# DeltaNet: beta and decays ahead of the first convolution; Q loaded back for its norms among the inverses; gates stored from ScalarE's queue

## The chip, the cores and the metric

The kernel runs on one core of a Trainium2 chip, as one program. The metric is the device time of one execution in microseconds (us); lower is better. Five engines work side by side, and each runs its own instructions strictly in the order in which they were written: TensorE (PE) multiplies matrices, VectorE (DVE) and ScalarE (ACT) work on elements, GpSimd (POOL) does some elementwise work, and SyncE (SP) mainly issues transfers (DMAs). ACT can issue transfers too, between its other instructions.

## What is computed

A decoder trunk of two layers on 16 meta tokens and 512 real ones with 1024 features: retention, then gated DeltaNet, each followed by a dense SwiGLU feed-forward network, all in float32. The change touches the DeltaNet layer alone. Cut to what matters, the reference has, for 8 heads with keys of 128 and values of 256 features:

```
qkv = silu(causal_conv(h @ w_in[qkv], conv_w))       # four taps along the tokens
q = l2norm(q) * DN_DK ** -0.5 ; k = l2norm(k)
beta = sigmoid(h @ w_in[beta])
g = -exp(a_log) * softplus(h @ w_in[a] + dt_bias)
# per chunk of tokens:
gam = cumsum(g) ; decay = exp(gam_i - gam_j) where i >= j
a_mat = strictly lower part of beta * (k k^T) * decay
u, w = triangular_solve(I + a_mat, [v * beta, k * beta * exp(gam)])
v_new = u - w @ state
o = (q * exp(gam)) @ state + ((q k^T) * decay) @ v_new
state = state * exp(g_last) + (k * exp(g_last - gam))^T @ v_new
y = (o / rms(o)) * norm_w * silu(h @ w_in[gate])   ;   out = y @ w_out
```

## The kernel before

Every large product splits both operands into a rounded part and a rest (`xhi`, `xlo` for the tokens, `whi`, `wlo` for the weights) and adds three products. A weight tile of 128x1024 is loaded by SP as `wraw`, cast to `whi` by ACT (line 179), and the rest `wlo` is formed by DVE (line 180); there are three buffers of each. TensorE multiplies at line 470 into a PSUM tile `g`, of which there are two. A weight tile's product with all 528 tokens is 48 matmuls of 264 columns.

The order of the instructions on each engine is fixed when the program is written: the code is a set of generators with due times (`spawn`, `tick`, the constants at the top), and a list scheduler then sets each engine's order. On the chip nothing is reordered.

The DeltaNet layer has these stages, in time: the keys and queries of 8 heads (`dn_keys`), the value products of the first heads, the gate products (`dn_silu_gate`), then the recurrence (`dn_states`, `dn_scan`) among further value and gate products.

- **Keys stage.** The products of head 0 are made as a pair (`gemm_pair`). Each product is scaled into `pad` by DVE (line 1202), convolved by ACT (first tap, line 1205) and DVE (three taps, line 1207), and passed through Silu on ACT (line 1210). The result goes to the DRAM scratch `d_kq` and is cast to `z` (line 460). For each head, the query's copy is also transposed by TensorE (`dn_norms`, line 1396, four transposes) and squared with a running sum by ACT (line 1400), which gives the query norms in `eq`.
- **Gates for beta and decay** (`dn_gates`). A product of 48 columns (line 1235), a few small products, a store to the scratch `d_g` and loads of it into tiles `zh` and `zl` per head, an addition on POOL (line 1356) that masks, and per head and chunk an exponential on ACT (line 1363), 32 in all. Silu and Exp sit in different tables of ACT, so each change from one to the other has an ACT_TABLE_LOAD.
- **Attention of a head** (`dn_attention`). Products of keys with keys and queries, which need `dec` (the exponentials) and `km`; they end in `d_mp`, the matrices to be inverted.
- **Inverse** (`dn_inverse`). All blocks are inverted at once by substitution on DVE (lines 1472 and 1478). The results go back to DRAM (`d_x`, `d_mp`, `d_m1`) by SP and ACT (lines 1496, 1497, 1501). Then `d_m1` is loaded into `rr` three times (line 1505, twice from SP and once from ACT's queue), cast to `um` by ACT (line 1506). The merge of the first two heads (`dn_merge`) loads `wh` from `d_x` (line 1515), transposes it on DVE into `wl` (line 1516) and multiplies on TensorE (line 1526) with `z`, loaded from `d_kq` and `d_mp` (lines 1720, 1721). ACT copies the product to `rh` (line 1534).
- **Output gates** (`dn_silu_gate`). 48 matmuls of 512 columns for each of two weight tiles, a scaling on DVE (line 1606), a Silu on ACT (line 1607) and a store to `d_sg` by SP (line 1608). Four of the eight gates stand ahead of the merge.

Of the kernel before, what the change touches and what calls it, by code (L numbers as in the profile page):

```python
# [10 lines left out]
AF = mybir.ActivationFunctionType  # L11
ALU = mybir.AluOpType
PSUM = bass.MemoryType.PSUM

P = 128
D = 1024
KT = D // P
NM = 16
NT = 512
T = NM + NT  # L20
HH = T // 2
EPS = 1e-6

RH = 4
DH = 8
# [18 lines left out]
TO_ATTEND = 7  # L44
ROWS = 5
POW = 5
NORMS = 18
ATTEND = 13
ATTEND_LAST = 8
ROWS_IN = (2, 10)  # L50
PAIRS_APART = 14
MASKED = 4
VALUES = 6
GATE_STEPS = (3, 6, 3)
GATES = [2, 2, 0, 2]
# [4 lines left out]
class Hybrid:  # L60
# [1130 lines left out]
    def conv_silu(self, w, x, rb, mt):  # L1191

        nc = self.nc
        p = self.psum_g()
        self.gemm(p, w, x, range(KT))
        return self.conv_evac(p, rb, mt)

    def conv_evac(self, p, rb, mt):
        nc = self.nc
        self.pads.reverse()  # L1200
        pad = self.pads[0]
        nc.vector.tensor_tensor(self.halves(pad[:, 3 : 3 + T]), p[:, :, :HH], self.halves(rb), op=ALU.mult)
        acc = self.t(self.tp, [P, T], "ra", bufs=4)
        cw = self.convw
        nc.scalar.activation(acc, pad[:, :T], AF.Copy, scale=cw[:, mt, 0:1])
        for i in range(1, 4):
            nc.vector.scalar_tensor_tensor(  # L1207
                acc, pad[:, i : i + T], cw[:, mt, i : i + 1], acc, op0=ALU.mult, op1=ALU.add
            )
        nc.scalar.activation(acc, acc, AF.Silu)  # L1210
        return acc

    def dn_gates(self, sp, x, rb):


        nc, a = self.nc, self.a
# [11 lines left out]
        pick = self.t(gp, [48, 16], "pick")  # L1228
        nc.vector.tensor_copy(pick, self.ident[:48, :16])
        nc.vector.tensor_copy(pick[32:48], self.ident[32:48, 32:48])  # L1230
        p = self.psum_g()
        for kt in range(KT):
            for i in range(2):
                for half in range(2):
                    nc.tensor.matmul(
                        p[:48, half, :HH],
                        wst[:, kt, :],
                        x[i][:, kt, half * HH : half * HH + HH],
                        start=kt == 0 and i == 0,
                        stop=kt == KT - 1 and i == 1,  # L1240
                    )
        ba = self.t(self.tp, [P, T], "ra", bufs=4)[:48]
        nc.vector.tensor_tensor(self.halves(ba), p[:48, :, :HH], self.halves(rb[:48, :]), op=ALU.mult)
        bm = self.t(self.tp, [P, 96], "am", bufs=1)
        nc.gpsimd.memset(bm, 0.0)
        self.spread(bm[:48], ba[:, :NM])
# [1 line left out]
        pt = self.psum_m()  # L1248
        for ch in range(5):
# [5 lines left out]
        ax, xa, e, z, z2, q = (  # L1255
            tmp[:, 80 + 40 * i : 120 + 40 * i].rearrange("p (a b) -> p a b", b=DH) for i in range(6)
        )
# [43 lines left out]
        pt = self.psum_m()  # L1301
# [6 lines left out]
        def rows_in(pair):  # L1308
            for hd in (2 * pair, 2 * pair + 1):
                self.dec[hd] = self.t(sp, [P, 4, P], ("zh", "zl")[pair % 2], bufs=3)  # L1310
                nc.sync.dma_start(self.dec[hd], by_head[hd, 1:].unsqueeze(0).to_broadcast([P, 4, P]))
# [5 lines left out]
        for dst, mat, meta in ((self.eglast, self.ones, self.ones[:NM, :]), (self.ekw, self.later, later3)):  # L1317
# [14 lines left out]
            op=ALU.mult,  # L1332
# [13 lines left out]
        for pair in range(DH // 2):  # L1346
            hds = (2 * pair, 2 * pair + 1)
            if pair == 1:
                yield PAIRS_APART
            if pair > 0:  # L1350
                while self.attended < 2 * (pair - 1):
                    yield 1
                rows_in(pair)
            yield ROWS_IN[pair > 0]
            for hd in hds:
                nc.gpsimd.tensor_tensor(
                    self.dec[hd], self.dec[hd], apart.unsqueeze(1).to_broadcast([P, 4, P]), op=ALU.add
                )
            yield MASKED
            for hd in hds:  # L1360
                for c in range(4):
                    o, de = (c + 1) * DH + hd, self.dec[hd][:, c]
                    nc.scalar.activation(de, de, AF.Exp, scale=-1.0, bias=sums[:, o : o + 1])
            self.decays = 2 * pair + 2

    def dn_keys(self, pool, hd, x, rb, first, gt):

        nc, a = self.nc, self.a
        for s, base in ((1, 0), (0, 8)):
            if first is None:  # L1370
                w = self.load_w(a["w_dqk"][hd, 1 - s])
                p = self.psum_g()
                self.gemm(p, w, x, range(KT))
            else:
                p = first.pop(0)
            t_ = self.conv_evac(p, rb, base + hd)
            real = t_[:, NM:].rearrange("p (c i) -> p c i", c=4)
            nc.sync.dma_start(self.d_kq[:, hd, :, s, :], real)
            if s == 1:
                zz = self.t(pool, [P, 2, 4, 2, P], "z", F32R)  # L1380
                zh, zl = zz[:, 0], zz[:, 1]
            self.split(zh[:, :, s, :], zl[:, :, s, :], real)
            if s == 0:
                nc.vector.tensor_copy(self.kmf[:, hd, :], t_[:, :NM])
            else:
                self.spawn(self.dn_norms(hd, t_), NORMS)
        return self.spawn(
            self.dn_attention(pool, hd, zh, zl, gt), ATTEND if hd < DH - 1 else ATTEND_LAST
        )

    def dn_norms(self, hd, t_):

        nc = self.nc
        pt = self.psum_m()
        for c in range(4):
            nc.tensor.transpose(pt[:, c * P : (c + 1) * P], t_[:, NM + c * P : NM + (c + 1) * P], self.ident)
        eq = self.eq[:, hd, :]
        for c in range(4):
            jk = self.t(self.sp, [P, P], "rh")
            nc.scalar.activation(jk, pt[:, c * P : (c + 1) * P], AF.Square, accum_out=eq[:, c : c + 1])  # L1400
        yield 1
        nc.vector.tensor_scalar(eq, eq, EPS, EPS * P, op0=ALU.add, op1=ALU.mult)

    def dn_attention(self, pool, hd, zh, zl, gt):

# [192 lines left out]
    def dn_silu_gate(self, hd, x, rb):  # L1598

        nc, a = self.nc, self.a  # L1600
        p = self.psum_g()
        ws = [self.load_w(a["w_dg"][hd, i]) for i in range(2)]
        for i in range(2):
            self.gemm(p, ws[i], x, range(KT), lo=NM, bank=i)
        sg = self.t(self.gp, [P, 2, NT], "sg", bufs=2)
        nc.vector.tensor_tensor(sg, p, rb[:, NM:].unsqueeze(1).to_broadcast([P, 2, NT]), op=ALU.mult)
        nc.scalar.activation(sg, sg, AF.Silu)
        nc.sync.dma_start(self.d_sg[:, hd], sg)

    def dn_scan(self, hd, z, vs, sp):  # L1610

# [152 lines left out]
    def deltanet(self, st, ctx, nxt):  # L1764
        nc, a = self.nc, self.a
        x = (st["hi"], st["lo"])
        self.gp = gp = self.pool(ctx, "dn", 1)
        self.sp = sp = self.pool(ctx, "scan", 2)
        op = self.pool(ctx, "og", 1)
# [26 lines left out]
        def gate(n):  # L1796
            for _ in range(n):
                self.dn_silu_gate(next(gates), x, rb)
# [7 lines left out]
        first = [self.psum_g() for i in range(2)]  # L1806
        self.gemm_pair(first, ws, x)
        self.finish(rows)
        rb = st["rb"]
        gt = self.spawn(self.dn_gates(sp, x, rb))  # L1810
        for hd in range(DH):
            att = self.dn_keys(sp, hd, x, rb, first if hd == 0 else None, gt)
            if hd in KEY_GATES:
# [1 line left out]
        self.dn_values(0, x, rb, sp)  # L1815
        self.finish(att)
        inv = self.spawn(self.dn_inverse(sp))
        self.dn_values(1, x, rb, sp)
        gate(FIRST_GATES)
        self.finish(inv)  # L1820
        self.spawn(self.dn_states(sp, op))
        for pair in range(4):
            gate(GATES[pair])
# [264 lines left out]
```

## Time and profile before

| | |
|---|---|
| median of 3 runs | 1669.75 us (1668.28 to 1670.8) |
| profiled execution | 1669.76 us, of which the span from first to last instruction is 1668.0 us |
| TensorE busy | 1643.1 us, 99% of the span |
| VectorE busy | 1297.6 us, 78% |
| ScalarE busy | 886.1 us, 53% |
| mean granted TensorE clock | 0.996 of full speed |

A share of busy time is an average over all stages. The DeltaNet layer runs from about 800 us on; its keys stage lies between 800 and about 905 us, the inverse between 937 and 1004 us.

### The profile page before, as it was taken

Reading aid. Unit: us, or ns where it says so; the run is one execution under the profiler, and the core shown is the slowest. Engines: PE = TensorE matmul, PEld = TensorE weight load, DVE = VectorE, ACT = ScalarE, POOL = GpSimd, SP = SyncE. Lnnn points to the kernel's source line nnn. Section 1 sums busy time; section 2 is a strip of 40 time slices with the busy share of each in tenths; the row PEclk is TensorE's granted clock in tenths of the full one; section 3 lists DMA queues with packets and bytes.
Section 4 is the critical chain, followed back from the end, with each engine's and each line's share of the span. In section 5 each row is a group of like instructions: output and inputs, shape, how many; then the busy total and the mean of one; then the engine's idle time right before and its main releaser. Section 6 shows DMA issues by size and latency. Waiting matters only on the chain.

```text
span 1668.0 us, 30777 instructions
## 1 busy us (share of the span) xinstructions
PE 1643.1 (99%) x12415; PEld 1550.9 (93%) x12415; DVE 1297.6 (78%) x2121; ACT 886.1 (53%) x1536; POOL 99.7 (6%) x139
## 2 busy tenths in 40 slices
PE   9999999999999999999989999999999999999998
PEld 9999999999999999999989988888877889999896
DVE  7886877798698887784689888796876798888672
ACT  5445555555345545543595427776663455555542
POOL 1000000000000000000030000010100000000010
PEclk9999999999999999999999999999999999999999
DMA  6564746565323332453354554432323223333451
GB/s 211 175 165 119 219 111 198 176 210 167 113 89 102 102 102 82 122 155 101 102 158 159 140 143 139 156 104 89 107 75 114 90 89 113 102 107 110 114 163 52
DMA packets 91888, 214.54 MB, mean 129 GB/s; under 512 B 20394, under 2 KB 42146, under 8 KB 90466
## 3 DMA queue, kind: packets, MB, share of 16 engines
q1 hardware_dynamic: 80066, 194.21, 35.3%
q0 software_dynamic: 4688, 16.53, 5.7%
q10 hardware_dynamic: 6992, 1.85, 0.5%
q8 instruction: 97, 1.59, 0.4%
q14 instruction: 45, 0.37, 0.1%
HBM read 190.30 MB, written 22.25 MB: 127 GB/s over the span
## 4 chain that ended last, share of the span: by engine, by line
PE 86%; DVE 9%; ACT 3%; issue 2%; POOL 1%; POOLq 0%; ACTq 0%; DVEq 0%
PE g L470 66%; PE m L470 14%; DVE wlo L461 1%; ACT whi L460 1%; DVE wsum L220 1%; DVE ra L1207 1%; PE m L573 0%; DVE flt L461 0%; POOL ss L1686 0%; PE m L559 0%; PE m L704 0%; DVE wlo L180 0%; DVE wraw L312 0%; DVE flb L461 0%; PE m L143 0%
## 5 line engine op out<-in xcount | busy, mean ns | idle before, releaser
L460 ACT CAST whi<-wraw 128x1024 fp32r<-128x1024 f32 x171 | 179.2, 1051 | 192.5 <-PE g L470 69.4
L470 PE MATMUL g<-fht,whi 128*128 128x264 f32 (+1 forms) x976 | 277.4, 284 | 0.8 <-DVE h L338 0.7
L470 PE MATMUL g<-fht,wlo 128*128 128x264 f32 (+1 forms) x976 | 276.1, 283 | 0.8 <-DVE wlo L461 0.8
L470 PE MATMUL g<-flt,whi 128*128 128x264 f32 (+1 forms) x976 | 275.9, 283 | 0.0
L470 PE MATMUL g<-xlo,whi 128*128 128x264 f32 (+1 forms) x1088 | 260.9, 306 | 0.0
L470 PE MATMUL g<-xhi,whi 128*128 128x264 f32 (+1 forms) x1024 | 251.8, 310 | 4.6 <-ACT whi L179 4.0
L470 PE MATMUL g<-xhi,wlo 128*128 128x264 f32 (+1 forms) x1024 | 251.2, 308 | 2.3 <-DVE wlo L180 2.3
L461 DVE TENSOR_TENSOR wlo<-wraw,whi 128x1024 fp32r<-128x1024 f32 x171 | 210.5, 1234 | 46.5 <-ACT whi L460 46.2
L179 ACT CAST whi<-wraw 128x1024 fp32r<-128x1024 f32 (+3 forms) x117 | 118.1, 1011 | 138.5 <-PE g L470 107.1
L470 PEld LDWEIGHTS g<-fht,whi 128*128 128x128 f32 x976 | 183.8, 188 | 1.3 <-ACT ra L540 0.9
L470 PEld LDWEIGHTS g<-fht,wlo 128*128 128x128 f32 x976 | 183.6, 188 | 1.1 <-DVE wlo L461 1.0
L470 PEld LDWEIGHTS g<-flt,whi 128*128 128x128 f32 x976 | 183.7, 188 | 0.5
L470 PEld LDWEIGHTS g<-xlo,whi 128*128 128x128 f32 x1088 | 176.7, 189 | 7.0 <-DVE xlo L529 0.2
L470 PEld LDWEIGHTS g<-xhi,whi 128*128 128x128 f32 x1024 | 167.8, 190 | 12.4 <-ACT whi L179 4.2
L470 PEld LDWEIGHTS g<-xhi,wlo 128*128 128x128 f32 x1024 | 167.3, 189 | 10.1 <-DVE wlo L180 3.3
L180 DVE TENSOR_TENSOR wlo<-wraw,whi 128x1024 fp32r<-128x1024 f32 (+3 forms) x117 | 138.0, 1180 | 40.5 <-ACT whi L179 39.5
L470 PE MATMUL g<-fhb,whi 128*128 128x264 f32 (+1 forms) x480 | 137.4, 286 | 0.0
L470 PE MATMUL g<-fhb,wlo 128*128 128x264 f32 (+1 forms) x480 | 136.1, 284 | 1.0 <-DVE wlo L461 0.8
L470 PE MATMUL g<-flb,whi 128*128 128x264 f32 (+1 forms) x480 | 135.7, 283 | 0.0
L461 DVE TENSOR_TENSOR wlo<-wsum,whi 128x1024 fp32r<-128x1024 f32 x54 | 66.1, 1225 | 44.5 <-ACT whi L460 44.5
L470 PEld LDWEIGHTS g<-fhb,wlo 128*128 128x128 f32 x480 | 90.3, 188 | 1.8 <-DVE wlo L461 1.8
L470 PEld LDWEIGHTS g<-flb,whi 128*128 128x128 f32 x480 | 90.3, 188 | 0.5
(562 smaller groups left out, 3804.4 us busy)
## 6 DMA issues: line engine op xcount, KB each, us to landing
wraw<-in_w_gu_dram SPq DMA_DIRECT2D x66, 512.0 KB, 3.4
wraw<-in_w_ret_dram SPq DMA_DIRECT2D x56, 512.0 KB, 3.7
sraw<-in_w_gu_dram SPq DMA_DIRECT2D x22, 512.0 KB, 4.1
wraw<-in_w_ret_dram POOLq DMA_DIRECT2D x18, 512.0 KB, 5.6
wraw<-in_w_dqk_dram SPq DMA_DIRECT2D x16, 512.0 KB, 3.4
wraw<-in_w_dv_dram SPq DMA_DIRECT2D x16, 512.0 KB, 3.3
wraw<-in_w_dg_dram SPq DMA_DIRECT2D x16, 512.0 KB, 3.9
wraw<-in_w_do_dram SPq DMA_DIRECT2D x16, 512.0 KB, 3.4
```

The source lines that it names most:

```text
L179: nc.scalar.copy(hi[:, c], raw[:, c])
L180: nc.vector.tensor_tensor(lo[:, c], raw[:, c], hi[:, c].bitcast(F32), op=ALU.subtract)
L220: nc.vector.scalar_tensor_tensor(dst[:, k, :], hh[:, kb + k, cs], g[:, kb + k : kb + k + 1], rb[:, cs], op0=ALU.mult, op1=ALU.mult)
L460: self.nc.scalar.copy(hi, src)
L461: self.nc.vector.tensor_tensor(lo, src, hi.bitcast(F32), op=ALU.subtract)
L470: mm(o, l, r[which], start=first and n == 0, stop=last and n == 2, **kw)
L1207: nc.vector.scalar_tensor_tensor(acc, pad[:, i : i + T], cw[:, mt, i : i + 1], acc, op0=ALU.mult, op1=ALU.add)
```

## The change

Three things are moved. First, `dn_gates` is made right behind the pair of products of head 0: the two products are scaled into their pads, then the 48-column product is made with two small PSUM tiles (`psum_m`) in place of a large one, and two steps of the generator are taken at once; the yield of 4 ticks ahead of the exponentials is gone. Second, the query norms leave the keys stage: `dn_norms` is spawned with the inverse, loads each head's queries back from `d_kq` (8 loads of 256 KB on SP's queue), and does the same transposes and squares; one DVE instruction in place of eight ends it. Third, the store of `d_sg` is issued by ACT in place of SP.

```diff
-NORMS = 18
+NORMS = 4
...
-MASKED = 4
...
-        return self.conv_evac(p, rb, mt)
-
-    def conv_evac(self, p, rb, mt):
-        nc = self.nc
+        return self.conv_taps(self.conv_pad(p, rb), mt)
+
+    def conv_pad(self, p, rb):
         self.pads.reverse()
         pad = self.pads[0]
-        nc.vector.tensor_tensor(self.halves(pad[:, 3 : 3 + T]), p[:, :, :HH], self.halves(rb), op=ALU.mult)
+        self.nc.vector.tensor_tensor(self.halves(pad[:, 3 : 3 + T]), p[:, :, :HH], self.halves(rb), op=ALU.mult)
+        return pad
...
-        p = self.psum_g()
+        p = [self.psum_m()[:48, :HH] for half in range(2)]
...
-        nc.vector.tensor_tensor(self.halves(ba), p[:48, :, :HH], self.halves(rb[:48, :]), op=ALU.mult)
+        for half in range(2):
+            hs = slice(half * HH, half * HH + HH)
+            nc.vector.tensor_tensor(ba[:, hs], p[half], rb[:48, hs], op=ALU.mult)
...
-            yield MASKED
...
-            else:
-                self.spawn(self.dn_norms(hd, t_), NORMS)
...
+    def dn_norms(self, sp):
+
+        nc = self.nc
+
+        def load(hd):
+            q = self.t(sp, [P, 4, P], "zh", bufs=3)
+            nc.sync.dma_start(q, self.d_kq[:, hd, :, 1, :])
+            return q
+
+        qs = [load(hd) for hd in range(2)]
+        for hd in range(DH):
+            yield NORMS
+            q = qs.pop(0)
+            if hd + 2 < DH:
+                qs.append(load(hd + 2))
+            pt = self.psum_m()
+            for c in range(4):
+                nc.tensor.transpose(pt[:, c * P : (c + 1) * P], q[:, c], self.ident)
+            eq = self.eq[:, hd, :]
+            for c in range(4):
+                jk = self.t(self.sp, [P, P], "rh")
+                nc.scalar.activation(jk, pt[:, c * P : (c + 1) * P], AF.Square, accum_out=eq[:, c : c + 1])
+            yield 1
+        nc.vector.tensor_scalar(self.eq, self.eq, EPS, EPS * P, op0=ALU.add, op1=ALU.mult)
...
-        nc.sync.dma_start(self.d_sg[:, hd], sg)
+        nc.scalar.dma_start(self.d_sg[:, hd], sg)
...
+        first = [self.conv_pad(p, rb) for p in first]
+        gt = self.dn_gates(sp, x, rb)
+        for _ in range(2):
+            next(gt)
+        self.spawn(gt, GATE_STEPS[1])
...
         inv = self.spawn(self.dn_inverse(sp))
+        norms = self.spawn(self.dn_norms(sp))
...
         self.finish(inv)
+        self.finish(norms)
```

What moves shows in the order of three places. The first is ACT in the keys stage. The names are those of the list above (`rh` is what a square writes, `zh` and `zl` are decays under their exponential, `ra` a convolution). Before, from the first exponential on:

```order
L1363 ACT_TABLE_LOAD
L1363 ACTIVATE zh_9498<-zh_9498,kl_9489 128x128 x4
L1363 ACTIVATE zh_9500<-zh_9500,kl_9489 128x128 x4
L1205 ACTIVATE ra_9705<-pad_01418_9154,convw_475 128x528
L1400 ACTIVATE rh_9741,eq_9146<-m_9734 128x128
L1400 ACTIVATE rh_9743,eq_9146<-m_9734 128x128
L1400 ACTIVATE rh_9745,eq_9146<-m_9734 128x128
L1363 ACTIVATE zl_9569<-zl_9569,kl_9489 128x128 x4
L1363 ACTIVATE zl_9571<-zl_9571,kl_9489 128x128 x4
L1210 ACT_TABLE_LOAD
L1210 ACTIVATE ra_9705<-ra_9705 128x528
```

In the changed kernel, the same stretch:

```order
L178 CAST whi_9888<-wraw_9886 128x1024
L1366 ACTIVATE zh_9464<-zh_9464,kl_9455 128x128 x4
L1366 ACTIVATE zh_9466<-zh_9466,kl_9455 128x128 x4
L1212 ACT_TABLE_LOAD
L1212 ACTIVATE ra_9584<-ra_9584 128x528
L1207 ACTIVATE ra_9687<-pad_01418_9154,convw_475 128x528
L459 CAST z_9502<-ra_9584 128x4x128
L1366 ACT_TABLE_LOAD
L1366 ACTIVATE zl_9710<-zl_9710,kl_9455 128x128 x4
L1207 ACTIVATE ra_9759<-pad_01417_9153,convw_475 128x528
L1212 ACT_TABLE_LOAD
L1212 ACTIVATE ra_9687<-ra_9687 128x528
```

The squares are gone from it. From behind `whi_9888` to the next weight cast, `whi_9966`, the changed order has 24 exponentials, 6 table loads, 3 Silus, 4 first taps and 3 casts to `z`.

The second is TensorE at the first merge. Before, behind the fourth gate (`g_11568`) stand all 48 matmuls of one value product (`g_11805`) and 27 of the next, whose last rows before the merge are:

```order
L470 MATMUL g_11940<-xlo_8689,whi_11801 128x264 x2
L470 MATMUL g_11940<-xhi_8688,wlo_11802 128x264 x2
L470 MATMUL g_11940<-xhi_8688,whi_11801 128x264 x2
L470 MATMUL g_11940<-xlo_8689,whi_11801 128x264
L1526 MATMUL m_11431<-wl_11410,z_11403 64x32 x8
L470 MATMUL g_11940<-xlo_8689,whi_11801 128x264
```

In the changed kernel the fourth gate is `g_11579`, and behind its last matmul stand:

```order
L469 MATMUL g_11579<-xhi_8688,wlo_11589 128x512
L1537 MATMUL m_11442<-wl_11421,z_11414 64x32 x8
L469 MATMUL g_11816<-xhi_8688,whi_11806 128x264 x2
L469 MATMUL g_11816<-xlo_8689,whi_11806 128x264 x2
L469 MATMUL g_11951<-xhi_8688,whi_11812 128x264 x2
L469 MATMUL g_11951<-xlo_8689,whi_11812 128x264
L469 MATMUL g_11816<-xhi_8688,wlo_11807 128x264 x2
L1537 MATMUL m_11459<-wl_11432,z_11417 64x32 x8
```

The value products have moved from ahead of the merge to behind it; the eight groups of norm transposes stand further up, among the value products of heads 0 and 1 and the gates.

The third is ACT at the same place. Before, the weight casts for the value products stand ahead of the load and the cast of `um`:

```order
L1607 ACTIVATE sg_11789<-sg_11789 128x1024
L179 CAST whi_11801<-wraw_11799 128x1024
L1205 ACTIVATE ra_11934<-pad_01418_9154,convw_475 128x528
L179 CAST whi_12096<-wraw_12094 128x1024
L1505 DMA rr_11364<-d_m_01405_9140 16x128
L179 CAST whi_12102<-wraw_12100 128x1024
L1521 COPY oq_11413<-wl_11410 32x4x32 x2
L1521 COPY oq_11424<-wl_11421 32x4x32 x2
L1534 COPY rh_11440<-m_11431 128x128
L1506 CAST um_9148<-rr_11364 96x128
```

In the changed kernel:

```order
L1618 ACTIVATE sg_11800<-sg_11800 128x1024
L1619 DMA d_sg_9139<-sg_11575 128x1024
L1516 DMA rr_11375<-d_m_01405_9140 16x128
L1532 COPY oq_11424<-wl_11421 32x4x32 x2
L1532 COPY oq_11435<-wl_11432 32x4x32 x2
L1619 DMA d_sg_9139<-sg_11800 128x1024
L1517 CAST um_9148<-rr_11375 96x128
L1545 COPY rh_11451<-m_11442 128x128
L178 CAST whi_11806<-wraw_11804 128x1024
L178 CAST whi_11812<-wraw_11810 128x1024
```

`whi_11806`, the cast for the first value product behind the merge, now stands behind `um`, which reads what the transfer into `rr` brings, and behind `rh`, which reads the merge. On SP the stores of `d_sg` are gone, and the eight loads of queries stand among the weight loads of the keys stage's second half and of the first gates.

## Rows read from the trace of the kernel before

**Rows 1.** The page's busy times by engine over the whole span.

```profile
PE 1643.1 (99%) x12415; PEld 1550.9 (93%) x12415; DVE 1297.6 (78%) x2121; ACT 886.1 (53%) x1536; POOL 99.7 (6%) x139
```

**Rows 2.** What TensorE waited for, whole run: total us, times, longest.

```profile
PE g L470 <- ACT whi L179: 4.0, 1, 4.0
PE g L470 <- DVE wlo L180: 2.3, 3, 1.4
```

**Rows 3.** Stretches: length, busy us of PE, PEld, DVE, ACT, POOL; granted clock.

```profile
850.00:855.00 5.00, 3.60 (x26) 3.00 (x24) 5.00 (x11) 4.36 (x13) 0.00 (x0) 1.00 0.56 191
855.00:860.00 5.00, 4.54 (x38) 4.54 (x39) 3.37 (x13) 4.94 (x8) 0.00 (x0) 1.00 0.34 115
860.00:865.00 5.00, 2.17 (x19) 1.93 (x17) 4.83 (x16) 4.96 (x9) 1.16 (x1) 1.00 0.04 13
865.00:870.00 5.00, 3.28 (x13) 2.98 (x14) 4.91 (x11) 4.98 (x13) 0.00 (x0) 0.59 0.72 189
870.00:875.00 5.00, 5.00 (x33) 5.00 (x33) 1.71 (x2) 4.85 (x7) 1.28 (x1) 0.73 0.84 235
```

**Rows 4.** Timeline, TensorE, 856 to 867 us: start, duration, what, idle before.

```profile
856.48 0.87 PE L470 MATMUL m<-z 128*128 128x256 f32 x6
857.18 0.41 PE L470 MATMUL g<-xhi,whi 128*128 128x264 f32 x2
857.43 0.40 PE L470 MATMUL g<-xlo,whi 128*128 128x264 f32 x2
...
866.17 0.81 PE L470 MATMUL g<-xhi,whi 128*128 128x264 f32 x2 [3.99 <-ACT whi L179]
```

**Rows 5.** Timeline, ScalarE, 859 to 866 us.

```profile
860.80 1.28 ACT L1363 ACTIVATE zh<-zh,kl 128x128 f32<-128x128 f32 x4
862.10 1.28 ACT L1210 ACT_TABLE_LOAD   x1
863.39 0.64 ACT L1210 ACTIVATE ra<-ra 128x528 f32<-128x528 f32 x1
863.94 0.72 ACT L1205 ACTIVATE ra<-pad,convw 128x528 f32<-128x528 f32 x1
864.57 0.60 ACT L460 CAST z<-ra 128x512 fp32r<-128x512 f32 x1
865.08 1.04 ACT L179 CAST whi<-wraw 128x1024 fp32r<-128x1024 f32 x1
866.02 0.26 ACT L1400 ACTIVATE rh<-m 128x128 f32<-128x128 f32 x1
```

**Rows 6.** Timeline, TensorE, 846 to 1002 us: norm transposes, fourth gate's end, merge.

```profile
846.66 0.60 PE L1396 MATMUL m<-ident,ra 128*128 128x128 f32 x4
847.02 0.49 PE L470 MATMUL g<-xhi,whi 128*128 128x264 f32 x2
...
990.50 0.39 PE L470 MATMUL g<-xhi,wlo 128*128 128x512 f32 x1
...
1001.67 0.65 PE L1526 MATMUL m<-wl,z 32*64 32x32 f32 x16
```

**Rows 7.** Timelines, VectorE, ScalarE and SP's queue, 990 to 1005 us.

```profile
990.93 1.22 DVE L1606 TENSOR_TENSOR sg<-g,rb 128x1024 f32<-128x1024 f32 x1 [1.19 <-PE g L470]
...
992.25 1.06 ACT L1607 ACTIVATE sg<-sg 128x1024 f32<-128x1024 f32 x1 [9.56 <-DVE sg L1606]
997.68 0.32 ACTq L1505 DMA_DIRECT2D rr<-d_m  x1
1004.42 0.30 ACT L1506 CAST um<-rr 96x128 fp32r<-96x128 f32 x1 [1.78 <-DMA rr<-d_m]
...
994.62 0.37 SPq L1721 DMA_DIRECT2D z<-d_mp  x1
```

**Rows 8.** Transfers, 985 to 1010 us: issues, KB each, median us to landing.

```profile
z<-d_mp SPq DMA_DIRECT2D x2, 512.0 KB, 3.9
...
rr<-d_m SPq DMA_DIRECT2D x2, 8.0 KB, 3.6
```

More of the change, by code (lines that the diff above doesn't have):

```diff
@@ L1195, in conv_silu, with conv_taps @@
         self.gemm(p, w, x, range(KT))
-        return self.conv_evac(p, rb, mt)
-    def conv_evac(self, p, rb, mt):
-        nc = self.nc
+        return self.conv_taps(self.conv_pad(p, rb), mt)
+    def conv_pad(self, p, rb):
         self.pads.reverse()
         pad = self.pads[0]
-        nc.vector.tensor_tensor(self.halves(pad[:, 3 : 3 + T]), p[:, :, :HH], self.halves(rb), op=ALU.mult)
+        self.nc.vector.tensor_tensor(self.halves(pad[:, 3 : 3 + T]), p[:, :, :HH], self.halves(rb), op=ALU.mult)
+        return pad
+    def conv_taps(self, pad, mt):
+        nc = self.nc
         acc = self.t(self.tp, [P, T], "ra", bufs=4)
@@ L1235, in dn_gates @@
                     nc.tensor.matmul(
-                        p[:48, half, :HH],
+                        p[half],
                         wst[:, kt, :],
@@ L1371, in dn_keys @@
                 w = self.load_w(a["w_dqk"][hd, 1 - s])
-                p = self.psum_g()
-                self.gemm(p, w, x, range(KT))
-            else:
-                p = first.pop(0)
-            t_ = self.conv_evac(p, rb, base + hd)
+                t_ = self.conv_silu(w, x, rb, base + hd)
+            else:
+                t_ = self.conv_taps(first.pop(0), base + hd)
             real = t_[:, NM:].rearrange("p (c i) -> p c i", c=4)
@@ L1389, in dn_keys @@
         )
-    def dn_norms(self, hd, t_):
+    def dn_norms(self, sp):
         nc = self.nc
[L1394 to L1402, printed above, removed]
+        def load(hd):
[17 more added lines that the diff above has]
+        nc.vector.tensor_scalar(self.eq, self.eq, EPS, EPS * P, op0=ALU.add, op1=ALU.mult)
     def dn_attention(self, pool, hd, zh, zl, gt):
@@ L1809, in deltanet @@
         rb = st["rb"]
-        gt = self.spawn(self.dn_gates(sp, x, rb))
+        first = [self.conv_pad(p, rb) for p in first]
[3 more added lines that the diff above has]
+        self.spawn(gt, GATE_STEPS[1])
         for hd in range(DH):
```

## The prediction

> **What bounds the kernel now.** I read the page's busy times first: TensorE is busy 1643.1 of 1668.0 us [rows 1], so the time is its work plus its gaps, some 25 us over the whole run, and nothing here removes work from it. Then the list of what TensorE waited for: the longest wait is one of 4.0 us for a `whi` cast, and three waits for `wlo` add 2.3 [rows 2]. Stretches of 5 us place the first: between 850 and 870 us TensorE is busy 3.60, 4.54, 2.17 and 3.28 of each 5 us, so it idles 6.41 us, and ScalarE is busy 4.36 to 4.98 in each [rows 3]. ScalarE is what this place waits for. The idle is not all: the granted clock falls to 0.59 and 0.73 in the two stretches from 865 to 875 [rows 3]. There 13 and 33 matmuls start. At full clock a pair of 264 columns starts every 0.245 us (857.18 to 857.43 [rows 4]); the stretch from 870 to 875 would hold some 41, and it has 33, about 1 us lost, and in the 3.3 busy us from 865 to 870 at a clock of 0.59 a further 1.4 to 2. I put the clock at 2.9 us and the keys stage's loss at 9.3 us in all. The timelines then show how the wait comes about: TensorE stands 3.99 us until 866.17 [rows 4], while ScalarE does exponentials, a table load, a Silu, a first tap and a cast before the `whi` cast at 865.08 [rows 5], all in the order in which they were written.
>
> **The change, keys stage.** Away from ScalarE go the squares, four of 0.26 us per head [rows 5], about 1.0 us each for the four or five heads that lie in this stretch. The gates come earlier by the 17 matmuls that stood ahead of them (2 us), and they no longer interrupt the pair's sequence. What is left I count from the changed order, between the casts `whi_9888` and `whi_9966`: 24 exponentials at 1.28/4 = 0.32 are 7.7 us, 6 table loads at 1.28 are 7.7, 3 Silus, from one start to the next 0.55 (863.39 to 863.94), 1.7, 4 first taps at 0.63 are 2.5, 3 casts at 0.51 are 1.5 [rows 5]: 21.1 us, and the cast itself 1.04. `whi_9888` waits for its buffer, which comes free when the product `g_9600` ends, and takes 1.04. So `whi_9966` stands 23.2 us behind that end. TensorE has in that time three products of 48 matmuls, 3 x 24 x 0.245 = 17.6 us, and two heads' attention, for each head two groups of six at 0.70 (856.48 to 857.18 [rows 4]) and some 0.2 for `km`: 3.2. That is 20.8, or 21.8 with gaps. It waits 1.4 to 2.4 us, and `wlo`, formed behind `whi`, adds about 0.8, as the shorter waits for it do now. With a drop of the clock as after the old wait, but in part, I take 3.5 us of loss in place of 9.3: a gain of 5.8. Bounds: if the exponentials start later (the masked sums on POOL must precede them), nearly all stays and the gain is 2; if nothing waits, it is 9.3.
>
> **The norms among the inverses.** The eight groups of transposes move from the keys to the products behind the last attention. A group costs TensorE 0.36 us (846.66 to 847.02 [rows 6]), 2.9 in all, with no sum changed. The squares, 8 us on ScalarE, have room: it idled 9.56 us in one piece before the Silu at 992.25 [rows 7]. The eight loads of queries are 2 MB more from DRAM on SP's queue; where a load waits for its buffer, the weight loads behind it wait too. No wait in rows 2 is for a weight's transfer, so I cost them at nothing while that lead holds; the nearest price without it is the 3.9 us of one 512 KB load [rows 8], once.
>
> **The gates' stores.** Eight issues leave SP and stand on ScalarE, 0.32 us each by its own issue of `rr` [rows 7], 2.6 us where it mostly waits. Seven I take as nothing. One counts: it stands ahead of the `rr` load, in the next sum.
>
> **The first merge.** This is where I expect the price. Before, TensorE ended the fourth gate at 990.73 and had 75 matmuls of value products before the merge at 1001.67 [rows 6]; all that the merge and `um` needed came in during those 10.9 us. In the changed order the merge follows the fourth gate's last matmul at once, and the value products behind it need `whi_11806`, which on ScalarE stands behind `um` and `rh`. Let G be the end of the fourth gate. The Silu of this gate starts 1.52 us after G (992.25) and ends 1.06 later [rows 7], at G+2.6. Behind it come a store's issue and the issue of `rr`, at about G+2.9 to G+3.2. It lands 3.6 us later by the median of the two from SP [rows 8], or 6.7 by the span from 997.68 to the cast at 1004.42, which waited for it [rows 7]: G+6.5 to G+9.9. Then `um` and `rh`, together about 0.5, and the cast, 1.04: TensorE gets its weights at G+8.0 to G+11.4. Is the merge itself ready? Its `z` was issued at 994.62 (G+3.9) [rows 7]; the inverse keeps its place while G moves back by the transposes' 2.9, so it is issued at G+1.0 and lands 3.9 later [rows 8], G+4.9. So the merge too is late, and it has 0.6 us of work. Of the time to G+8.0 to 11.4, TensorE uses this 0.6: an idle of 7.4 to 10.8 us. `wlo` behind it adds 0.3 to 0.6. The clock, which after 4 us of idle cost 2.9 in the keys stage, costs 1.5 to 2.9 again. The wait of 1.4 us for `wlo` [rows 2], which lay among the 75 matmuls, goes. Sum: +7.8 to +12.9; I take +10.2, near the middle, since the transfers around it are about as dense as before.
>
> The Trainium skill, page "DMA: Bandwidth & Descriptors", section "Anatomy of one DMA", puts the fixed part of a small transfer at about 2 us, mostly the receipt of the write. The row says 3.6 and more for 8 KB [rows 8], so the trace does not agree here; by the page's figure `rr` would land at about G+5.2, the merge's `z` would come about as late, the cast would end near G+7, and the term would be an estimated +7, the time some 1671: rival 2, below.
>
> **Sum.** 1669.76 - 5.8 + 10.2 = 1674.2 us. The profiled execution lies on the median of the runs (1669.75), so nothing has to be shifted.
>
> **The rivals.** (1) *The merge is hidden after all.* If the fourth gate ends later against the inverse than I think, or `rr` lands fast, `um` is there when ScalarE comes to it. But the Silu, `um`, `rh` and the cast still lie in a row behind G: 2.6 + 0.3 + 0.5 + 1.04 = G+4.4, an idle of 3.8 at the least, without a drop of the clock, less 1.4: +2.4. With the full gain of 5.8 to 9.3 this gives 1663 to 1666.5. It decides once `rr` is in by G+4. For it: SP's two loads of `rr` took only 3.6. Against it: the third can't be issued before G+2.9. (2) *The two cancel.* A merge of +6 to +8 against a gain of 5 to 8: 1667 to 1672.5, within 0.2%. For it: all bounds overlap there. (3) *The keys stage stays bound by ScalarE.* Six table loads and 24 exponentials in one piece are as much as before; if POOL's sums or a late weight cast push them 2 to 3 us back, the wait and the low clock stay, the gain is 2, and with +10 to +13 at the merge the time is 1678 to 1681. (4) *A load of queries holds SP's queue* until its buffer is free, and the next weight tile is late: 4 us on top, 1678; nothing in the rows shows SP late.
>
> **How the numbers follow.** What a measurement of this kernel can tell from no change is about 0.2%, 3.3 us: 1666.4 to 1673.1. My forecast (keys gain about 6, merge +8 to +13, so 1672 to 1677) has 0.45, of which a fifth lies within 0.2%. Rival 1 has 0.17, nearly all faster. Rival 2 has 0.18. Rival 3 has 0.14 and rival 4 0.06, both slower. Slower: 0.36 + 0.14 + 0.06 = 0.56; the same: 0.09 + 0.18 = 0.27; faster 0.17. The predicted time is 1674. The range leaves about 0.1 at either end: low, half of rival 1 falls out, 1665.5; high, the upper half of rival 3, 1679.5.
>
> **What would show it.** Right: between 850 and 870 us TensorE's idle falls from 6.4 to 2 to 4 us and no line-1400 square stands there; behind the fourth gate, around 990 us, the merge waits for `z` or `wl`, and the next value product waits 3 to 6 us for `whi`, with `um` ahead of it waiting for the transfer of `rr`, and a lower granted clock after it. Wrong: a merge with no gap around it (rival 1), a `whi` wait of 4 us left in the keys stage (rival 3), a wait for a weight's transfer (rival 4), or a new gap in the later recurrence, where the orders differ here and there and I expect none.

## The result and the profile after

The changed kernel takes 1684.53 us (median of 6 runs, 1683.39 to 1688.38) against 1670.72 for the kernel before (6 runs, 1668.28 to 1672.21): the ratio is 1.0082, 95% interval 1.0071 to 1.0093. It is slower, as forecast, but by 13.8 us where 4.4 were forecast, and outside the range given (to 1679.5). The profiled execution of the changed kernel is the longest of its runs, 1688.38 us with a span of 1686.6; a second profile of it (last run below) lies at its median.

What TensorE waited for in the whole run of the changed kernel (total us, times, longest), against [rows 2]:

```profile
PE g L469 <- ACT whi L178: 9.6, 2, 8.2
PE m L1435 <- DVE km L615: 3.0, 1, 3.0
PE m L1537 <- DMA z<-d_mp: 2.3, 1, 2.3
```

The one wait of 4.0 us for `whi` is gone, and one of 8.2 has come. Where it stands is shown by TensorE's timeline at the merge (line 1537 is now the merge's), and by ScalarE's (line 1618 is the gate's Silu, 1619 its store, 1516 the load of `rr`, 1517 the cast to `um`, 1545 the copy to `rh`, 178 the weight cast):

```profile
991.60 0.39 PE L469 MATMUL g<-xhi,wlo 128*128 128x512 f32 x1
994.33 0.65 PE L1537 MATMUL m<-wl,z 32*64 32x32 f32 x16 [2.33 <-DMA z<-d_mp]
1003.18 0.81 PE L469 MATMUL g<-xhi,whi 128*128 128x264 f32 x2 [8.20 <-ACT whi L178]
...
1016.46 0.64 PE L469 MATMUL g<-xhi,wlo 128*128 128x264 f32 x2
...
1018.34 0.40 PE L469 MATMUL g<-xlo,whi 128*128 128x264 f32 x2
```

```profile
993.29 1.06 ACT L1618 ACTIVATE sg<-sg 128x1024 f32<-128x1024 f32 x1 [6.20 <-DVE sg L1617]
993.35 0.34 ACTq L1619 DMA_DIRECT2D d_sg<-sg  x1
993.79 0.61 ACTq L1516 DMA_DIRECT2D rr<-d_m  x1
994.44 0.30 ACT L1532 COPY oq<-wl 32x128 f32<-32x128 f32 x1
994.59 0.81 ACTq L1619 DMA_DIRECT2D d_sg<-sg  x1
994.75 0.91 ACT L1532 COPY oq<-wl 32x128 f32<-32x128 f32 x3
1001.73 0.30 ACT L1517 CAST um<-rr 96x128 fp32r<-96x128 f32 x1 [6.06 <-DMA rr<-d_m]
1001.93 0.26 ACT L1545 COPY rh<-m 128x128 f32<-128x128 f32 x1
1002.09 2.94 ACT L178 CAST whi<-wraw 128x1024 fp32r<-128x1024 f32 x3
```

TensorE ends the fourth gate at about 992, waits 2.33 us for the merge's `z`, and then 8.20 for a weight cast which stands on ScalarE behind `um`; ScalarE itself stands 6.06 us before the transfer of `rr`, issued at 993.79, 7.9 us before the cast. Before, 75 matmuls of value products lay in this place. The last two lines of TensorE's timeline belong to the clock, below.

The stretches around it have the same columns as [rows 3]:

```profile
990.00:995.00 5.00, 2.64 (x25) 1.87 (x23) 1.64 (x3) 1.60 (x3) 0.00 (x0) 1.00 0.71 185
995.00:1000.00 5.00, 0.00 (x0) 0.00 (x0) 0.00 (x0) 0.64 (x3) 0.00 (x0) 0.65 0.88 286
1000.00:1005.00 5.00, 1.82 (x8) 1.81 (x9) 2.40 (x5) 3.27 (x5) 0.00 (x0) 0.50 0.66 209
1005.00:1010.00 5.00, 5.00 (x80) 4.29 (x79) 1.66 (x2) 2.26 (x9) 0.00 (x0) 0.50 0.91 314
1010.00:1015.00 5.00, 5.00 (x33) 4.29 (x33) 0.47 (x3) 2.13 (x6) 0.00 (x0) 0.50 0.21 83
1015.00:1020.00 5.00, 4.99 (x34) 4.81 (x34) 3.46 (x9) 2.27 (x7) 0.00 (x0) 0.80 0.00 0
```

From such stretches a loss can be worked out: 5 us less the busy time times the granted clock. Here these are 2.4, 5.0, 4.1, 2.5, 2.5 and 1.0: 17.5 us, of which 10.5 are idle and some 7 are lost because TensorE works at 1.2 GHz in place of 2.4 (clock 0.50). TensorE went back to work at 1003.2, and the clock was back at full speed only at about 1017: a pair of 264 columns lasts 0.64 us at 1016.46 and 0.40 at 1018.34. Before, the same sum from 975 to 1030 us gives 1.4.

In the keys stage the loss by this sum is 9.3 us before and 10.1 in this profile. The stretches of the changed kernel that have most of it:

```profile
835.00:840.00 5.00, 3.92 (x33) 3.71 (x31) 3.62 (x6) 4.03 (x10) 5.00 (x4) 1.00 0.88 224
840.00:845.00 5.00, 3.10 (x17) 2.91 (x18) 4.77 (x9) 4.45 (x9) 4.93 (x3) 0.79 0.59 200
...
855.00:860.00 5.00, 3.06 (x24) 2.64 (x22) 4.85 (x13) 4.97 (x12) 0.00 (x0) 1.00 0.33 86
860.00:865.00 5.00, 4.07 (x18) 4.07 (x19) 5.00 (x12) 4.98 (x7) 0.00 (x0) 0.50 0.69 207
865.00:870.00 5.00, 5.00 (x37) 5.00 (x36) 3.47 (x11) 2.41 (x6) 1.17 (x1) 0.82 0.88 318
```

ScalarE's timeline at the start of it shows what was new there (line 1366 is the exponential, 1360 the masked sum on POOL):

```profile
831.39 1.05 ACT L178 CAST whi<-wraw 128x1024 fp32r<-128x1024 f32 x1 [3.56 <-PE g L469]
834.73 1.28 ACT L1366 ACTIVATE zh<-zh,kl 128x128 f32<-128x128 f32 x4 [2.29 <-POOL zh L1360]
836.96 1.28 ACT L1366 ACTIVATE zh<-zh,kl 128x128 f32<-128x128 f32 x4 [0.94 <-POOL zh L1360]
...
857.65 1.03 ACT L178 CAST whi<-wraw 128x1024 fp32r<-128x1024 f32 x1
```

The squares are gone, but ScalarE now stands 3.23 us before POOL's sums, with three Silus, four first taps and the next weight cast behind it. That cast ends 27.3 us after the start of the one at 831.39, where I had counted 23.2. TensorE's waits in this stage are these:

```profile
841.89 0.41 PE L1435 MATMUL m<-km 128*96 128x96 f32 x2 [2.98 <-DVE km L615]
...
858.73 0.51 PE L469 MATMUL g<-xhi,whi 128*128 128x264 f32 x2 [1.42 <-ACT whi L178]
...
860.93 0.81 PE L469 MATMUL g<-xhi,wlo 128*128 128x264 f32 x2 [1.45 <-DVE wlo L179]
```

The longest is not for a weight but for `km`, which VectorE makes from what the first of these Silus brings (it stands 1.50 us before that Silu). So POOL's sums hold TensorE by way of the Silu behind the exponentials too.

### The profile page after: what moved, and what is told of

Read it like the earlier page. It is cut to its first block, busy times and chain, and to the rows that moved or that the text cites. A ratio compares the mean times of both kernels' runs of the same rounds, so it can differ in the third digit from the quotient of the medians.

```text
span 1686.6 us, 30774 instructions
## 1 busy us (share of the span) xinstructions
PE 1652.2 (98%) x12415; PEld 1559.0 (92%) x12415; DVE 1295.5 (77%) x2115; ACT 882.9 (52%) x1534; POOL 102.6 (6%) x139
## 4 chain that ended last, share of the span: by engine, by line
PE 82%; DVE 10%; ACT 3%; issue 2%; DMA 2%; POOL 1%; ACTq 0%; POOLq 0%; DVEq 0%
PE g L469 64%; PE m L469 13%; DVE wlo L460 2%; ACT whi L459 1%; DVE flt L460 1%; DVE wraw L311 1%; DVE wsum L219 1%; DVE flb L460 1%; POOL ss L1697 1%; DVE wlo L179 0%; DMA rr<-d_m 0%; DMA h<-d_sg 0%; DMA xlo<-d_o 0%; PE m L703 0%; PE m L572 0%
```

## The experiments

All ratios are to runs of the kernel before on the same chip, and the losses are the sums described above from each kernel's own profile. They are collected here, worked out from stretches of 5 us. They do not hold everything: the profile of the stores alone is 3.8 us longer than that of before (spans of 1671.8 and 1668.0), with the same losses in both places.

```
                                   ratio to before        keys stage        first merge
                                   (95% interval)         800 to 910 us     975 to 1030 us
                                                          loss (idle)       loss (idle)
before                             1                       9.3 (6.6)         1.4 (1.4)
changed                            1.0082 (1.0071-1.0093) 10.1 (5.8)        17.5 (10.5)
changed, again                     1.0076 (1.0060-1.0092)  5.9 (4.5)        16.6 (9.6)
gates only                         0.9968 (0.9955-0.9981)  7.6 (4.9)         2.3 (2.3)
norms only                         0.9982 (0.9973-0.9991)  2.4 (2.4)         6.2 (3.5)
stores only                        1.0001 (0.9989-1.0014)  9.2 (6.5)         1.4 (1.4)
norms and stores                   1.0041 (1.0025-1.0057)  2.4 (2.4)        17.6 (9.8)
gates and norms                    1.0006 (0.9996-1.0017)  5.3 (4.1)         6.4 (3.5)
changed, norms 12 apart            0.9977 (0.9966-0.9988)  5.7 (4.3)         0.0 (0.0)
norms only, 12 apart               0.9953 (0.9938-0.9968)  1.0 (1.0)         1.4 (1.4)
changed, yield back                1.0045 (1.0028-1.0061)  2.3 (2.3)        15.1 (8.3)
changed, um cast on POOL           1.0061 (1.0045-1.0077)  6.2 (3.5)        16.5 (9.4)
changed, rr from SP                1.0039 (1.0023-1.0056)  6.9 (4.1)         6.0 (4.6)
changed, yield back, 12 apart      0.9943 (0.9929-0.9958)  1.4 (1.4)         0.0 (0.0)
```

My theory after the result was that two places decide: the merge, where norms and stores together make an order without cover, and the keys stage, where the early exponentials wait for POOL. The rivals were that the earlier gates, the loads of the queries or the stores on ScalarE cost by themselves.

**The parts one by one.** First the gates alone (the diff's `conv_pad`, `psum_m`, `next(gt)` and the missing yield; norms as before, stores on SP):

```diff
+first = [self.conv_pad(p, rb) for p in first]
+gt = self.dn_gates(sp, x, rb)
+for _ in range(2):
+    next(gt)
...
 else:
     self.spawn(self.dn_norms(hd, t_), NORMS)
```

> The kernel before with the first part of the change alone: beta and decays ahead of the first convolution, the yield ahead of the exponentials gone; norms stay in the keys stage, stores on SP. The first merge keeps its 75 matmuls of value products ahead of it. Theory (the price of the change lies at the first merge, and is made by norms and stores together): no wait of over 2 us around the merge, and the keys stage no better than before, since ScalarE's exponentials now wait for POOL's sums: time 1668 to 1676. Rival A (the earlier gates are what costs): 1680 or more. Rival B (the earlier gates do gain in the keys stage, and the merge hides it): 1662 to 1666.

Measured: 1667.98 us against 1672.62, ratio 0.9968. The time lies between the theory and rival B, and the gain of 0.32% points to rival B: taken alone, the earlier gates help. Rival A is out. The 4.0 us wait for `whi` is gone from the keys stage, one of 3.7 for `vs` on VectorE has come, and the loss there falls by 1.7 only. The profile is that of the slowest of this kernel's runs (1670.04), so where the rest of the gain lies was not seen.

The norms alone:

```diff
-            else:
-                self.spawn(self.dn_norms(hd, t_), NORMS)
...
+        norms = self.spawn(self.dn_norms(sp))
...
+        self.finish(norms)
```

> The kernel before with the second part alone: queries loaded back and normed among the inverses. The order puts 8 matmuls between the fourth gate and the merge, and the weight casts for the value products ahead of the cast of um. Theory: the merge waits 2 to 4 us for its transfers, with some clock lost behind it, and no wait of 8 us for whi; the keys stage gains 3 to 6 us by the squares that left it: 1666 to 1675. Rival C (the loads of queries or the transposes themselves cost): 1680 or more, with waits elsewhere than at the merge.

Measured: 1669.84, ratio 0.9982. The time is the theory's: the keys stage gives back 6.9 us, more than expected, and the merge costs 4.8 more than before. The wait there is this, for a weight cast and not, as expected, for the merge's own transfers; 8 matmuls and not 75 were at hand:

```profile
PE g L470 <- ACT whi L179: 3.4, 1, 3.4
```

Rival C is out: the eight loads and the transposes cost nothing that shows elsewhere.

The stores alone:

```diff
-        nc.sync.dma_start(self.d_sg[:, hd], sg)
+        nc.scalar.dma_start(self.d_sg[:, hd], sg)
```

> The kernel before with the third part alone: the gates' stores issued by ScalarE. 69 matmuls stand between the fourth gate and the merge. Theory: 1668 to 1673, no change, since a store's issue is 0.3 to 0.8 us on an engine that waits there. Rival D (stores on ScalarE's queue slow the transfers of the inverse by themselves): 1676 or more.

Measured: 1673.16 against 1672.62, ratio 1.0001. No change; rival D is out.

**Norms and stores together** (both diffs above on the kernel before):

> The second and third part together, gates as before. The order at the merge is that of the changed kernel: no matmul between the fourth gate and the merge, um and rh ahead of the weight casts. Theory: an idle of about 10 us behind the fourth gate and half the clock for some 13 us behind that, +14 to +17 at this place, less 3 to 6 gained in the keys stage: 1678 to 1686. Rival A would have it near 1670.

Measured: 1680.16, ratio 1.0041. The merge loses 17.6 us, as in the changed kernel, though one part alone costs 4.8 there and the other nothing:

```profile
PE g L470 <- ACT whi L179: 7.5, 1, 7.5
...
PE m L1536 <- DMA z<-d_mp: 1.9, 1, 1.9
```

So the price is made by the two together: not by their work, but by the order that the scheduler makes of them.

**Gates and norms, stores on SP:**

```diff
-        nc.scalar.dma_start(self.d_sg[:, hd], sg)
+        nc.sync.dma_start(self.d_sg[:, hd], sg)
```

> The first and second part together, stores on SP as before: 8 matmuls between the fourth gate and the merge, and the weight casts ahead of um. Theory (norms and stores together make the bad order; the parts add up otherwise): the place of the merge loses about 6 us as with the norms alone, the keys stage 6 to 10: 1667 to 1674. Rival (the norms alone in the presence of the early gates make the stall): 1680 or more.

Measured: 1672.45 against 1671.74, ratio 1.0006: the theory's side. The merge loses 6.4 as with the norms alone. But in the keys stage gates and norms do not add up: 5.3 is lost together, and 2.4 with the norms alone. With the norms gone, the early gates take back 3 of the 7 us that the norms give, though alone they gained.

**One number.** The whole change with the norms spawned further apart, so that the order at the merge is another:

```diff
-NORMS = 4
+NORMS = 12
```

> The whole change with one number altered: the norms spawned 12 ticks apart in place of 4. The order then has 20 matmuls of a value product between the fourth gate and the merge, the cast whi_11806 ahead of the last gate's Silu and um behind two weight casts. The keys stage is that of the changed kernel. Theory: the loss behind the fourth gate, 17.5 us in the changed kernel (10.5 of idle, 7.0 of low clock), falls to 1 to 5; the keys stage still loses about 10: 1669 to 1674. Rival C (the loads of queries or the stores on ScalarE cost by themselves): still 1680 or more.

Measured: 1668.04 against 1671.9, ratio 0.9977. That is a little under the expected 1669 to 1674, as the keys stage loses 5.7 us here and not about 10. Nothing of the merge's loss is left: 20 matmuls ahead of it, and two weight casts ahead of `um`, were enough. All loads, squares and stores are still there; rival C falls a second time.

The same number with the norms as the only part:

> The second part alone, with the norms 12 ticks apart; gates and stores as before. Between the fourth gate and the merge stand 31 matmuls, and two weight casts ahead of the last Silu. Theory: the keys stage loses 2.4 us as in the run of the second part alone, against 9.3 before, and the merge 1 to 4 against 6.2 in that run: 1661 to 1666, faster than both. Rival: where the gain of that run came from something else than the keys stage, no better than 1668.

Measured: 1663.69, ratio 0.9953, inside the expected 1661 to 1666.

**The exponentials' place.** The changed kernel with the yield put back:

```diff
+            yield MASKED
             for hd in hds:
                 for c in range(4):
                     o, de = (c + 1) * DH + hd, self.dec[hd][:, c]
```

> The changed kernel with the yield of 4 ticks ahead of the exponentials put back, nothing else. ScalarE's order then has 16 exponentials and one cast to z fewer ahead of the weight cast whi_9966, in place of 24. Theory (in the keys stage ScalarE stood behind POOL's masked sums with all the exponentials ahead of the weight cast): the keys stage's loss falls from 10.1 to 5 to 8 us, the merge's stays near 17: 1679 to 1683. Rival (the exponentials' place doesn't matter): as the changed kernel, 1684 to 1686.

Measured: 1679.91, ratio 1.0045. The loss in the keys stage falls to 2.3, further than expected. ScalarE's next weight cast starts early enough although the first exponentials still wait for POOL:

```profile
831.35 1.05 ACT L179 CAST whi<-wraw 128x1024 fp32r<-128x1024 f32 x1 [3.55 <-PE g L470]
833.24 1.28 ACT L1368 ACTIVATE zh<-zh,kl 128x128 f32<-128x128 f32 x4 [0.84 <-POOL zh L1361]
835.54 1.28 ACT L1368 ACTIVATE zh<-zh,kl 128x128 f32<-128x128 f32 x4 [1.02 <-POOL zh L1361]
...
848.12 1.03 ACT L179 CAST whi<-wraw 128x1024 fp32r<-128x1024 f32 x1
```

It is 17.8 us from the start of the one cast to the end of the next, against 27.3: 16 exponentials and 4 table loads lie between them here, 24 and 6 in the changed kernel. What counts is how many of them the order puts ahead of the weights.

**What ScalarE stands before.** The changed kernel with the cast of `um` on POOL:

```diff
-        nc.scalar.copy(self.um, um)
+        nc.gpsimd.tensor_copy(self.um, um)
```

> The changed kernel with one instruction on another engine: the cast of um is made by POOL, so ScalarE doesn't stand before the transfer of rr; the order of TensorE at the merge is the same. Theory: the weight cast follows the merge's copy at once, TensorE idles 4 to 6 us in place of 10.5 and loses 2 to 4 in place of 7.0 by the clock: 1673 to 1678. Rival E (it is the transfers of wh and z that the merge itself waits for, not um): the idle stays at 9 or more, 1682 to 1686.

Measured: 1682.22, ratio 1.0061: a miss. The idle is 9.4, where I expected 4 to 6, but not for rival E's reason:

```profile
PE g L469 <- DVE wlo L179: 5.2, 1, 5.2
PE g L469 <- ACT whi L178: 2.3, 1, 2.3
PE m L1537 <- DMA z<-d_mp: 1.9, 1, 1.9
```

(These are the waits from 975 to 1030 us.) ScalarE was free, and `whi` came. The wait moved to VectorE, where the subtraction that makes `um`'s last part (and the copies of it) stands ahead of `wlo`:

```profile
1000.23 0.28 DVE L1518 TENSOR_TENSOR um<-rr,um 32x128 fp32r<-32x128 f32 x1 [8.59 <-POOL um L1517]
1000.55 0.28 DVE L615 CAST u<-um 96x48 fp32r<-96x48 f32 x2
1000.75 3.48 DVE L179 TENSOR_TENSOR wlo<-wraw,whi 128x1024 fp32r<-128x1024 f32 x3
```

So the theory had to be widened: the transfer of `rr` holds two engines, and both stand ahead of the weights.

**The transfer itself.** All three loads of `rr` from SP, none behind the gate's store on ScalarE's queue:

```diff
-            (nc.sync, nc.scalar)[b % 2].dma_start(um[32 * b : 32 * b + NM], self.d_m1)
+            nc.sync.dma_start(um[32 * b : 32 * b + NM], self.d_m1)
```

> The changed kernel with one transfer moved: all three loads of rr are issued by SP, none by ScalarE behind the 512 KB store of the gate. No value product stands ahead of the merge, as in the changed kernel, but the first weight cast now stands ahead of um on ScalarE and the first wlo ahead of um on VectorE. Theory (the reader of rr stands ahead of the weights on both engines, and rr lands late behind the store): the 10.5 us of idle shrink to 4 to 6 (the merge's z, then one cast), the clock's loss to 2 to 5: 1673 to 1679. Rival E (the merge's own transfers): idle stays at 9 or more, 1682 to 1686.

Measured: 1679.13, ratio 1.0039, a little above the upper end of the expectation. The idle is 4.6 and the loss 6.0; the waits from 975 to 1030 us are:

```profile
PE m L1537 <- DMA z<-d_mp: 2.2, 1, 2.2
PE g L469 <- ACT whi L178: 2.1, 1, 2.1
```

The third load landed 3.2 to 3.6 us after its issue, like the other two, where ScalarE's took 7.9. But the order also put one weight cast and one `wlo` ahead of `um`, so the earlier landing and the other order are not told apart by this run; that both engines were held by `rr` agrees with it. The profiled execution (1676.69) is among the faster of this kernel's runs (1676.06 to 1683.52); what its slower runs lose was not seen.

**Both cures, and the changed kernel again.** The yield and the number together:

> The whole change with the yield ahead of the exponentials put back and the norms 12 ticks apart. Theory: both cures add: the keys stage loses about 2, the merge about 1: 1661 to 1666. Rival (the gain of the yield was a matter of one profile): as with the norms 12 ticks apart alone, 1667 to 1670.

Measured: 1663.05, ratio 0.9943: 0.57% faster than before, with 1.4 us lost in the keys stage and nothing at the merge. It is the lowest ratio of all.

> The changed kernel itself once more, for its profile: the first one was that of the longest of its runs, and two kernels with the same order in the keys stage lost 6.2 and 5.7 us there, not 10.1. Theory: 1682 to 1686, with about 17 us lost behind the fourth gate again, and 5 to 7 in the keys stage where the run is near the median. Rival: 10 in the keys stage again.

Measured: 1684.73, ratio 1.0076. The merge loses 16.6 in this profile, and the keys stage 5.9 and not 10.1. ScalarE waits less for POOL here:

```profile
833.37 1.28 ACT L1366 ACTIVATE zh<-zh,kl 128x128 f32<-128x128 f32 x4 [0.53 <-POOL zh L1360]
835.67 1.28 ACT L1366 ACTIVATE zh<-zh,kl 128x128 f32<-128x128 f32 x4 [1.01 <-POOL zh L1360]
```

The order is the same instruction for instruction. TensorE's wait for `km` is 0.8 us and not 3.0. So the 10.1 of the first profile was partly that execution's, the longest of its kernel.

## Why the prediction was wrong

**The sign and the place were right.** The prediction said that the price would be at the first merge, that the merge would wait for its `z`, ScalarE for `rr` and TensorE for `whi` behind `um`; all three waits are in the rows, and the run with the norms 12 apart takes them away and the price with them. That the idle came out in its range (10.5 and 9.6 us, for 7.4 to 10.8) was partly luck. ScalarE issued `rr` 2.0 us after the fourth gate's end, while its Silu still ran, and not 2.9 to 3.2; but the load took 7.9 and 6.9 us, longer than both bounds (3.6 and 6.7). SP issued the load of `z` that I had put 1.0 us behind the gate's end 1.7 us ahead of it (990.16), so the merge waited 2.3 us only, and the wait for `whi` was 8.2 and 7.3 and not 3 to 6.

**The step that failed is the merge's term, and in it the price of the clock.** For the clock I carried over "1.5 to 2.9", the loss behind the 4.0 us wait of the keys stage. It is 6.9 us in the first profile and 7.0 in the second. Behind the old gap of 3.99 us in the keys stage the clock stood at 0.50 for some 6 us of work [rows 3, 4]; behind this one for 13.7, in both profiles. The whole term measured +16.1 and +15.2, where I took +10.2 and at most +12.9. The other runs show the clock's loss over several sums of idle: 3.5 us of idle came with 2.7 to 2.9 (norms only; gates and norms), 8.3 with 6.8, 9.4 with 7.1, 9.8 with 7.8, and 4.6 in two pieces with 1.4. So it is 6.8 to 7.8 wherever the idle is 8.3 us or more, and there it does not grow with the idle. What makes the low stretch longer stays open. Two things go together in these runs: there is more idle (in the run with the yield back in two gaps of 3.1 and 4.7), and the work behind it is another. Behind the gap of 3.99 us TensorE had only matmuls of 264 columns until the clock rose; behind the long ones it had most of the first merge's small ones as well (80 matmuls from 1005 to 1010 us, against 33 from 870 to 875 [rows 3]). No run changed one without the other.

**The keys stage's gain was taken too large.** I forecast 3.5 us of loss in place of 9.3, a gain of 5.8. In the second profile it is 5.9 (a gain of 3.4), in the first 10.1 (a loss of 0.8). The wait for `whi` that I forecast, 1.4 to 2.4 us, is there: 1.4 and 2.4. Missing from the sum were the wait for `km`, 3.0 and 0.8, and the size of the clock's loss, 4.2 and 1.5. My count from `whi_9888` to `whi_9966`, 23.2 us, also left out ScalarE's own waits for POOL, 1.5 to 3.2 us, which I had only as a bound. And the parts do not add up as I had it: the norms' leaving gives 6.9 us by itself, and the earlier gates, which I took as help, then take 3 of it back, with 24 exponentials ahead of the weights. With the yield the loss is 2.3.

**Steps that held.** The stores' issue costs nothing by itself (1.0001), the loads of queries and the squares among the inverses cost nothing that shows (norms 12 apart: 0.9953), and TensorE never waited for a weight's transfer, so rival 4 is out. Rival 1 is out for the change as it is, and is what the change with one other number does. Rival 2 is out (its terms give 1667.8 to 1672.8, not quite the range written). Rival 3's sign, a `whi` wait of 4 us left in the keys stage, did not come, though in the first profile the stage lost as much as before; its time, 1678 to 1681, was too low for the same reason as the forecast.

**The sum with measured terms** (second profile): keys -3.4, merge +15.2, and from 1030 to 1400 us +1.5 (losses of 9.3 in place of 7.8): +13.3 us, where the medians differ by 13.8 and the spans of the profiles by 15.1. Some 2 us of the spans' difference have no place in these sums.

The Trainium skill, page "DMA: Bandwidth & Descriptors", section "Anatomy of one DMA", gives a small transfer about 2 us of fixed cost; its figures are of transfers that GpSimd issues, while these were issued by SP and ScalarE. The runs reach that figure once: 8 KB from SP took 3.1 to 4.6 us, and from ScalarE's queue 2.2 to 8.0. The estimate of 1671 us that the prediction works out from it had the load too short.

## What to carry to other kernels

A change of order is worth what stands ahead of the waits that it leaves: read in the new order which instructions cover each transfer, and on every engine that feeds the product, not on one. Price a gap of TensorE as idle plus what is lost at the low clock behind it, and don't carry that over from a gap of another size with other work behind it: here 4 us of idle cost 7 in one place, and 10 cost 17 in another. Where a scheduler sets the order, parts that are harmless alone (0.9982 and 1.0001) can cost together (1.0041), and one number may undo it.

## What the runs showed of the hardware that was not expected

An idle of 9.6 to 10.5 us of TensorE was followed by 13.7 us of work at a granted clock of 0.50, against some 6 us behind an idle of 4.0. The clock's loss was near 7 us (6.8 to 7.8) for every idle from 8.3 to 10.5 us.

A load of 8 KB issued on ScalarE's queue landed 5.1 to 8.0 us later in all eight profiles that have its landing and in which it was issued behind SP's three loads of `z`, 512 KB each, also where no store stood ahead of it on its own queue (7.0 with the stores on SP). Where it was issued ahead of two or all three of these loads, it landed 2.2 to 4.0 us later (stores alone, and the two orders of the change with the norms 12 apart). In the changed kernel `rr` was issued at 993.79, behind these issues of `z`, and took what the last line says:

```profile
991.58 0.42 SPq L1731 DMA_DIRECT2D z<-d_kq  x1
992.05 0.51 SPq L1732 DMA_DIRECT2D z<-d_mp  x1
...
rr<-d_m ACTq DMA_DIRECT2D x1, 8.0 KB, 7.9
```

With the stores alone it was issued at 995.84, ahead of loads of `z` at 996.57, 997.99 and 998.45, and took 2.2 us.

The same load from SP, ahead of two of the three in every order, took 3.1 to 4.6. So ScalarE's queue does not make it slow by itself; it was late where larger transfers had been issued before it, on whichever queue. That these are the cause was not tried by itself.
